# Reordering the products of a pair of k-blocks in a split-precision encoder block: high weight parts first, low parts last

## The chip, the cores and the metric

The kernel runs on one core of one Trainium2 chip. A core has a matrix engine (TensorE), a vector engine (VectorE), an activation engine (ScalarE), a general engine (GpSimd, POOL in the profile) and a queue that issues transfers (SyncE, SP). The metric is device time in microseconds (us) of one execution, lower is better. The median of three runs before the change is 2034.01 us (2033.57 to 2034.16).

## The reference, cut to what matters

One layer of an encoder: 256 tokens, width 4096, everything in float32. Five large weight matrices are streamed once.

```python
xn = rms_norm(h, norm_in_g[i])
proj = xn @ w_in[i]                          # 4096 x 14336
q, k, v, z_a, a_c, g_c, z_c = jnp.split(proj, ..., axis=-1)
y_a = chunked_attention(q, k, v, rel_table[i])
y_a = rms_norm(y_a, attn_out_g[i]) * jax.nn.silu(z_a)
y_c = conv_module(a_c, g_c, ..., w_pw[i], b_pw[i])   # 2048 x 2048 inside
y_c = rms_norm(y_c, conv_out_g[i]) * jax.nn.silu(z_c)
h = h + jnp.concatenate([y_a, y_c], axis=-1) @ w_out[i]        # 4096 x 4096
gate = jax.nn.sigmoid(rms_norm(h, ple_norm_g[i]) @ w_ple_gate[i] + b_ple_gate[i])
h = h + gate * (p[i] @ w_ple[i])
return rms_norm(h, final_g)
```

## The kernel before, in words

**Split products.** A float32 operand is held as the sum of a high part (a rounded format that TensorE multiplies in one pass) and a low part (what the rounding left). A product x @ w is then three matmuls: high x with high w, low x with high w, high x with low w, called kinds 0, 1 and 2 in the helper `add` (lines 378 to 389). The weight's high part is a cast by ScalarE (line 204), its low part a subtraction by VectorE that needs the high part (line 205); both are made in `parts_of`. There are three buffers each for high parts (`wh`) and low parts (`wl`), five for raw weights (`wt`), and two each for the parts of sums of blocks (`uh`, `ul`). A buffer comes free when its last reader is done. In a matmul the block of x (128 by 128) is the stationary operand, loaded by an instruction of its own (PEld in the profile), and 512 columns of w stream through it.

**Products.** `mixed_product` computes two column blocks of 512 for both halves of the tokens (256 tokens are two blocks of 128 rows), over all k-blocks in pairs. It holds four accumulators of 128 by 512, one bank each, with the names P2, P4, P3 and X; the pool `ps_acc` has four buffers, so the next product's four accumulators take the banks of this one. A *unit* of its list is one pair of k-blocks, done in one of two ways:
- a plain step: 8 block products, 24 matmuls, written by `add_plain` for one k-block and then the other; per block in the order of the column block j, the token half h, the kind;
- a seven-product step (marked `*` or `+` in the lists): a Strassen-like scheme with seven block products (P1, P5, P7, P2, P3, P6, P4), 21 matmuls, at the price of sums of weight blocks `ua` and `ub` on VectorE (lines 465 to 473; for `+` the first is formed by two transfers, one with accumulation, lines 418 and 419). P1, P5, P6 and P7 go to four helper banks of the pool `ps_tmp`.

The lists (`dense`, `early`, `first`, `late` and so on, lines 329 to 338) begin and end with plain steps. The first nine steps of the first product are written out in `first_pairs` by hand, with pinned order; the last product holds its last three pairs back and finishes them in pinned order (`add_left`).

**Reading out.** When a product ends, VectorE reads the four accumulators in the order of `QUARTERS` (P2, P4, P3, X) and combines each with sums from the helper banks: line 535 for scaled pairs, 1028 and 1030 for the pointwise product, 1054 for the gates, 1138 for the output projection, 1180 for the last gate. There are 25 such products on the four `ps_acc` banks: 9 scaled pairs (convolution inputs, queries and keys, values), 2 single value blocks by `product` (line 229), 2 pointwise, 4 gates, 4 of the output projection, 4 of the last gate; three of the last four are followed by `product` calls in `ps_tmp`.

**Order.** Except where `pin` keeps the program's order, a planner orders each engine's instructions when the program is built: it steps through a model of the engines, gives an engine the ready instruction that stands earliest in the program, and assigns a buffer when its tile is first written. So the program's order is a priority, and each engine's order is fixed before the run. On the chip each engine waits by semaphores for what its next instruction needs. Work that can be put off (convolution taps, normalisation) lies in a list `later`, of which `fill` issues a few after each step.

Of the kernel before, what the change touches and what calls it, by code (L numbers as in the profile page):

```python
# [25 lines left out]
def hybrid_block(  # L26
# [25 lines left out]
    NH = T // P  # L52
# [129 lines left out]
    def fill(n):  # L182
        for _ in range(min(n, len(later))):
            later.popleft()()
# [11 lines left out]
    def part_tiles():  # L196
        return [wpool.tile([P, KC, NB], F32R, tag=tag, name=tag, bufs=3) for tag in ("wh", "wl")]

    def parts_of(wt, kc, tiles=None):
        if tiles is None:  # L200
            tiles = part_tiles()
        wh, wl = tiles
        made = (
            nc.scalar.copy(wh[:, :kc, :], wt[:, :kc, :]),  # L204
            nc.vector.tensor_tensor(  # L205
                wl[:, :kc, :], wt[:, :kc, :], wh[:, :kc, :].bitcast(F32), ALU.subtract
            ),
        )
        recent[:] = made
        return (wh, wl), made  # L210
# [108 lines left out]
    def pair_parts(src):  # L319

        tiles = [upool.tile([P, 2, NB], F32R, tag=tag, name=tag) for tag in ("uh", "ul")]
        return parts_of(src, 2, tiles)[0]
# [17 lines left out]
    def mixed_product(  # L340
        w, col, lhs, comb, order, on_helpers, ahead=None, fills=(0,), on_begin=None, apart=NB,
# [36 lines left out]
        def add(name, x, w2, n, final, kinds=range(3), then=lambda ins: None):  # L378

            for kind in kinds:  # L380
                a, b = ((x[0], w2[0]), (x[1], w2[0]), (x[0], w2[1]))[kind]
                made.append(
                    nc.tensor.matmul(  # L383
                        banks[name], a, b, start=name not in begun,
                        stop=final and ends[name] == n and kind == 2 and not (left and name in "P2 P3 P4"),
                    )
                )
                begun.add(name)
                then(made[-1])

        def block(kb, h):
            t = lhs[kb // 4]
            return [t[:, kb % 4, q, h * P : (h + 1) * P] for q in range(2)]

        def add_plain(n, k, wh, wl, **kw):
            pair = order[n][0]
            for j in range(2):
                for h in range(NH):
                    name = (("P2", "P3"), ("P4", "X"))[h][j]
                    add(name, block(2 * pair + k, h), (wh[:, j], wl[:, j]), n, k == 1, **kw)  # L400

        sums = {}

        def sums_ahead(n):
# [22 lines left out]
        for n, (pair, seven) in enumerate(order):  # L427
# [4 lines left out]
            wts = []  # L432
            for k in range(2):
                wt = wpool.tile([P, 2, NB], F32, tag="w", name="wt")
# [10 lines left out]
                fill(fills[n % len(fills)])  # L445
                continue
            if not seven:
                for k in range(2):
                    add_plain(n, k, *parts_of(wts[k], 2)[0])
                fill(fills[n % len(fills)])  # L450
                continue
            begins = not helper
# [7 lines left out]
            w0h, w0l = parts_of(w0, 1)[0]  # L460
# [6 lines left out]
            with queued_behind(before if seven == "+" else ()):  # L467
                uah, ual = pair_parts(ua)
            w1h, w1l = parts_of(w1, 2)[0]
# [7 lines left out]
            def s_of(i):  # L477
                t, at = comb[pair] if isinstance(comb, dict) else (comb[pair // 4], pair % 4)
                return [t[:, at + i // 2, q, (i % 2) * P : (i % 2 + 1) * P] for q in range(2)]

            k0, k1 = 2 * pair, 2 * pair + 1
            add("P1", block(k0, 0), (w0h[:, 0], w0l[:, 0]), n, True)
            add("P5", s_of(1), (uah[:, 0], ual[:, 0]), n, True)
            add("P7", s_of(0), (uah[:, 1], ual[:, 1]), n, True)
            add("P2", block(k1, 0), (w1h[:, 0], w1l[:, 0]), n, True)
            add("P3", s_of(3), (w1h[:, 1], w1l[:, 1]), n, True)
            add("P6", s_of(2), (ubh[:, 0], ubl[:, 0]), n, True)
            add("P4", block(k1, 1), (ubh[:, 1], ubl[:, 1]), n, True)
            if begins and on_begin:
# [31 lines left out]
    def scaled_pair(w, col, apart, order, r, fills, home={}, **kw):  # L521

        t, z = [], []

        def on_helpers(helper):
            for dst, src in zip((t, z), sum_tiles(**home)):
                dst.extend(src)
            nc.scalar.activation(z[0][0], helper["P1"], AF.Identity, scale=r[:, :1])
            helper_sums(helper, z)
            for h, j in QUARTERS[1:]:  # L530
                nc.scalar.activation(z[h][j], z[h][j], AF.Identity, scale=r[:, h : h + 1])

        c = mixed_product(w, col, xT, xS, order, on_helpers, fills=fills, apart=apart, **kw)
        for h, j in QUARTERS:
            stt(
                z[h][j], c[h][j], r[:, h : h + 1], z[h][j],
                ALU.mult, ALU.subtract if j else ALU.add,
            )
        return t
# [682 lines left out]
    for j in range(2):  # L1222
        wt = wpool.tile([P, 2, NB], F32, tag="w", name="wt")
# [115 lines left out]
```

## Time and profile before

| what | value |
|---|---|
| median of three runs | 2034.01 us |
| profiled execution, its own time | 2032.83 us |
| its span, first to last instruction | 2031.1 us |
| mean granted TensorE clock | 0.998 |
| instructions | 26144 |
| TensorE matmuls, weight loads | 9094, 9094 |
| from HBM | 430.77 MB, 214 GB/s over the span |

In the profile PE is TensorE's matmuls, PEld its weight loads, DVE VectorE, ACT ScalarE, POOL GpSimd; L383 is line 383 of the kernel. Windows and starts are in us from the span's start. A group's row gives count, busy us, mean ns of one, then the engine's idle time just before and who ended it. A matmul's drawn length covers its way through the array, and the next one starts before it ends: the distance between starts is the rate.

### The profile page before, as it was taken

The numbers are of one execution on the slowest core, as the hardware profiler recorded it, in microseconds if no ns is written. First come the engines' busy times: TensorE is split into PE (matmuls) and PEld (weight loads), VectorE is DVE, ScalarE is ACT, GpSimd is POOL, SyncE is SP. The second block draws the span as 40 slices with busy tenths as digits, with TensorE's granted clock in tenths as the row PEclk, the third lists the DMA queues.
The fourth block names the chain that finished last, engine by engine and source line by source line (L and its number), as shares of the span: only waits on it lengthen the run. The fifth ranks groups of instructions, "written<-read, shape, count | busy, mean of one in ns | idle before, by whom it ended". The sixth has DMA issues, their size and how long they took to land.

```text
span 2031.1 us, 26144 instructions
## 1 busy us (share of the span) xinstructions
PE 2015.5 (99%) x9094; PEld 1658.7 (82%) x9094; DVE 1871.1 (92%) x2658; ACT 1203.3 (59%) x1568; POOL 46.0 (2%) x50
## 2 busy tenths in 40 slices
PE   9999999999999999999999999999999999999997
PEld 7888888888888888888888888888888888888876
DVE  7999999679999986868899999999999999999998
ACT  7655555655655445676556566675665666665555
POOL 0000000000000000000000000000000000000000
PEclk9999999999999999999999999999999999999999
DMA  8787878688678867556666666676666656666765
GB/s 294 223 237 233 257 214 251 191 245 239 188 217 250 254 187 207 171 185 205 194 214 198 202 205 214 217 229 209 206 213 201 208 187 207 204 220 205 234 208 179
DMA packets 171167, 436.69 MB, mean 215 GB/s; under 512 B 13966, under 2 KB 17182, under 8 KB 171034
## 3 DMA queue, kind: packets, MB, share of 16 engines
q1 hardware_dynamic: 161952, 417.93, 64.0%
q0 software_dynamic: 8432, 16.25, 4.9%
q8 instruction: 71, 1.16, 0.2%
q10 hardware_dynamic: 650, 0.84, 0.1%
q14 instruction: 62, 0.51, 0.1%
HBM read 430.77 MB, written 4.19 MB: 214 GB/s over the span
## 4 chain that ended last, share of the span: by engine, by line
PE 92%; DVE 5%; issue 2%; ACT 1%; DMA 1%; POOLq 0%; POOL 0%; ACTq 0%; DVEq 0%
PE acc L383 67%; PE acc_P L383 16%; PE acc L229 5%; DVE wl L205 2%; PE tmp_ps L170 1%; DVE cv L721 1%; DMA wt<-in_w_out_dram 0%; PE tmp_ps L890 0%; DVE ul L205 0%; PE tmp_ps L874 0%; PE tmp_ps L908 0%; PE tmp_ps L913 0%; ACT wh L204 0%; PE acc L371 0%; DVE cv L799 0%
## 5 line engine op out<-in xcount | busy, mean ns | idle before, releaser
L383 PE MATMUL acc<-wh,big_t 128*128 128x512 f32 x3992 | 1234.7, 391 | 0.7 <-DVE y_c L1030 0.3
L204 ACT CAST wh<-wt 128x1024 fp32r<-128x1024 f32 (+1 forms) x737 | 713.4, 978 | 550.5 <-PE acc L383 365.0
L205 DVE TENSOR_TENSOR wl<-wt,wh 128x1024 fp32r<-128x1024 f32 (+1 forms) x737 | 821.8, 1127 | 82.0 <-ACT wh L204 78.6
L383 PEld LDWEIGHTS acc<-wh,big_t 128*128 128x128 f32 x3992 | 746.8, 188 | 155.1 <-issue 0.9
L383 PE MATMUL acc<-wl,big_t 128*128 128x512 f32 x1996 | 770.7, 391 | 0.6 <-DVE wl L205 0.5
L383 PEld LDWEIGHTS acc<-wl,big_t 128*128 128x128 f32 x1996 | 374.3, 188 | 79.5 <-DVE wl L205 2.3
L204 ACT CAST uh<-ua 128x1024 fp32r<-128x1024 f32 x160 | 168.3, 1052 | 80.9 <-DVE ua L466 46.1
L721 DVE SCALAR_TENSOR_TENSOR cv<-uT,dw,cv 128x250 f32<-128x250 f32 (+19 forms) x480 | 202.3, 463 | 1.1
L205 DVE TENSOR_TENSOR ul<-ua,uh 128x1024 fp32r<-128x1024 f32 x160 | 194.9, 1218 | 8.4 <-ACT uh L204 8.0
L383 PE MATMUL acc_P<-uh,big_t 128*128 128x512 f32 x516 | 157.9, 391 | 0.0
L204 ACT CAST uh<-ub 128x1024 fp32r<-128x1024 f32 x92 | 96.8, 1053 | 95.8 <-DVE ub L473 86.5
L205 DVE TENSOR_TENSOR ul<-ub,uh 128x1024 fp32r<-128x1024 f32 x92 | 112.2, 1220 | 6.1 <-ACT uh L204 5.2
L383 PEld LDWEIGHTS acc_P<-uh,big_t 128*128 128x128 f32 x516 | 95.8, 188 | 22.3 <-ACT uh L204 3.1
L383 PE MATMUL acc_P<-ul,big_t 128*128 128x512 f32 x258 | 98.8, 391 | 0.1
L229 PE MATMUL acc<-wh,big_t 128*128 128x512 f32 x304 | 93.9, 390 | 0.0
L465 DVE TENSOR_TENSOR ua<-wt 128x512 f32<-128x512 f32 x95 | 65.1, 685 | 18.3 <-DMA wt<-in_w_in_dram 12.4
L383 PE MATMUL acc<-uh,big_t 128*128 128x512 f32 x252 | 78.1, 390 | 0.0
L383 PE MATMUL acc_P<-wh,big_t 128*128 128x512 f32 x252 | 77.8, 389 | 0.0
L229 PEld LDWEIGHTS acc<-wh,big_t 128*128 128x128 f32 x304 | 56.9, 188 | 11.9 <-issue 0.2
L383 PE MATMUL acc_P<-uh,comb_t 128*128 128x512 f32 x216 | 66.4, 390 | 0.1
L466 DVE TENSOR_TENSOR ua<-wt 128x512 f32<-128x512 f32 x95 | 64.9, 683 | 1.1 <-DMA wt<-in_w_in_dram 1.1
L473 DVE TENSOR_TENSOR ub<-ub,wt 128x512 f32<-128x512 f32 x92 | 63.0, 685 | 0.8
(250 smaller groups left out, 1589.3 us busy)
## 6 DMA issues: line engine op xcount, KB each, us to landing
wt<-in_w_in_dram SPq DMA_DIRECT2D x416, 512.0 KB, 4.5
wt<-in_w_out_dram SPq DMA_DIRECT2D x128, 512.0 KB, 4.3
wt<-in_w_ple_gate_dram SPq DMA_DIRECT2D x128, 512.0 KB, 4.2
wt<-in_w_pw_dram SPq DMA_DIRECT2D x32, 512.0 KB, 4.7
ua<-in_w_in_dram SPq DMA_DIRECT2D x31, 512.0 KB, 4.2
ua<-in_w_in_dram POOLq DMA_DIRECT2D x31, 512.0 KB, 8.3
wt<-in_w_in_dram SPq DMA_DIRECT2D x31, 256.0 KB, 2.7
hc<-in_x_dram SPq DMA_DIRECT2D x8, 512.0 KB, 4.8
```

What stands on the lines that cost most here:

```text
L170: nc.tensor.transpose(pt[:, i * T + h * P : i * T + (h + 1) * P], src[:, h, b] if len(src.shape) == 4 else src[:, h, b * P : (b + 1) * P], ...
L204: nc.scalar.copy(wh[:, :kc, :], wt[:, :kc, :]),
L205: nc.vector.tensor_tensor(wl[:, :kc, :], wt[:, :kc, :], wh[:, :kc, :].bitcast(F32), ALU.subtract),
L229: nc.tensor.matmul(acc, a, b[:, k, :], start=kb == 0 and kind == 0, stop=kb == kblocks - 1 and kind == 2,)
L383: nc.tensor.matmul(banks[name], a, b, start=name not in begun, stop=final and ends[name] == n and kind == 2 and not (left and name in "P2 ...
L465: plus(ua[:, 0], w0[:, 0], w0[:, 1])
L466: plus(ua[:, 1], w0[:, 1], w1[:, 1])
L473: plus(ub[:, 1], ub[:, 0], w1[:, 0])
L721: nc.vector.scalar_tensor_tensor(cv[:, i, PAD - k :], uT[:, i, : T + k - PAD], dw[:, b, k : k + 1], cv[:, i, PAD - k :], ALU.mult, ALU.add,)
```

## The change

The products of a pair of k-blocks are put in another order. In plain steps a new function `add_pair` takes the place of two calls of `add_plain`: first all 16 matmuls that read high parts of both blocks, then the 8 that read low parts; the loops run over block, token half, kind and column block, so that the two column blocks of one stationary operand follow each other. In seven-product steps the five products P1, P2, P3 (of raw blocks) and P5, P7 (of the first sum) are done with their high parts first (P1, P2, P3, then P5, P7) and then with their low parts in the same order; P6 and P4 follow as before. `add_plain` stays for the pinned first steps. The parts themselves, the buffers and the transfers are made by the same code in the same order.

```diff
+        def add_pair(n, parts):
+
+            pair = order[n][0]
+            for kinds in ((0, 1), (2,)):
+                for k, (wh, wl) in enumerate(parts):
+                    for h in range(NH):
+                        for kind in kinds:
+                            for j in range(2):
+                                name = (("P2", "P3"), ("P4", "X"))[h][j]
+                                add(name, block(2 * pair + k, h), (wh[:, j], wl[:, j]), n, k == 1, (kind,))
...
             if not seven:
-                for k in range(2):
-                    add_plain(n, k, *parts_of(wts[k], 2)[0])
+                add_pair(n, [parts_of(wt, 2)[0] for wt in wts])
                 fill(fills[n % len(fills)])
                 continue
...
-            add("P1", block(k0, 0), (w0h[:, 0], w0l[:, 0]), n, True)
-            add("P5", s_of(1), (uah[:, 0], ual[:, 0]), n, True)
-            add("P7", s_of(0), (uah[:, 1], ual[:, 1]), n, True)
-            add("P2", block(k1, 0), (w1h[:, 0], w1l[:, 0]), n, True)
-            add("P3", s_of(3), (w1h[:, 1], w1l[:, 1]), n, True)
+            raw = (
+                ("P1", block(k0, 0), (w0h[:, 0], w0l[:, 0])),
+                ("P2", block(k1, 0), (w1h[:, 0], w1l[:, 0])),
+                ("P3", s_of(3), (w1h[:, 1], w1l[:, 1])),
+            )
+            two = (
+                ("P5", s_of(1), (uah[:, 0], ual[:, 0])),
+                ("P7", s_of(0), (uah[:, 1], ual[:, 1])),
+            )
+            for group, kinds in ((raw, (0, 1)), (two, (0, 1)), (raw, (2,)), (two, (2,))):
+                for product_of in group:
+                    add(*product_of, n, True, kinds)
             add("P6", s_of(2), (ubh[:, 0], ubl[:, 0]), n, True)
             add("P4", block(k1, 1), (ubh[:, 1], ubl[:, 1]), n, True)
```

## The prediction

> **What bounds the kernel now.** I read the page's busy times first, then the chain, then the engines by stretch, to see whether TensorE is short of work anywhere. The next two fences are lines of the page (busy time and share; the chain by engine; the costliest group: count, busy us, mean ns, idle before it) and the busy times by stretch.
>
> ```profile
> PE 2015.5 (99%) x9094; PEld 1658.7 (82%) x9094; DVE 1871.1 (92%) x2658; ACT 1203.3 (59%) x1568; POOL 46.0 (2%) x50
> PE 92%; DVE 5%; issue 2%; ACT 1%; DMA 1%; POOLq 0%; POOL 0%; ACTq 0%; DVEq 0%
> L383 PE MATMUL acc<-wh,big_t 128*128 128x512 f32 x3992 | 1234.7, 391 | 0.7 <-DVE y_c L1030 0.3
> ```
>
> ```profile
> 0.00:50.00 50.00, 48.70 (x234) 38.57 (x235) 36.40 (x61) 36.45 (x70) 0.88 (x8) 1.00 0.86 294
> 50.00:1980.00 1930.00, 1928.49 (x8681) 1588.90 (x8680) 1793.47 (x2537) 1140.44 (x1460) 43.29 (x40) 1.00 0.69 214
> 1980.00:2031.00 51.00, 38.32 (x183) 31.27 (x181) 41.28 (x61) 26.37 (x39) 1.86 (x2) 0.92 0.52 179
> 1200.00:1300.00 100.00, 100.00 (x443) 82.71 (x442) 95.19 (x114) 58.96 (x65) 0.00 (x0) 1.00 0.63 205
> ```
>
> TensorE carries 92% of the chain. Of its 15.6 us of idle time, 14.0 lie in the first 50 us and the last 51 us, which the change does not reach; 1.5 are left between. The granted clock there is 1.00. A busy TensorE can still hide delay, though, because a matmul is drawn 391 ns long while the next starts sooner. So I looked at one place where it did wait (matmuls, VectorE, weight loads; start, length, and in brackets the idle time with who ended it):
>
> ```profile
> 838.51 1.98 PE L383 MATMUL acc<-wh,big_t 128*128 128x512 f32 x8
> 841.01 1.20 PE L383 MATMUL acc<-wl,big_t 128*128 128x512 f32 x4 [0.53 <-DVE wl L205]
> 839.75 2.35 DVE L205 TENSOR_TENSOR wl<-wt,wh 128x1024 fp32r<-128x1024 f32 x2
> 841.01 0.77 PEld L383 LDWEIGHTS acc<-wl,big_t 128*128 128x128 f32 x4 [0.95 <-DVE wl L205]
> ```
>
> Eight starts in 1.98 - 0.39 us make a pitch of 0.227 us for seven steps. The ninth matmul was due at 838.51 + 8 x 0.227 = 840.33 and started at 841.01: 0.68 us lost. The next three take 0.81 us instead of 0.68: a restart costs 0.13 more. Also, eight products with high parts stand in a row here, against the program's order (two high, one low): the planner already pulls high products forward where it sees a low part late. The change writes by hand what the planner does in need.
>
> **The change part by part.** No instruction is added or removed: 9094 matmuls, 9094 loads, the same casts and subtractions, the same DMAs on SP's and POOL's queues in the same program order. What moves is when parts are needed and when buffers and banks come free. I count in matmuls of 0.227 us; the lists of units give 214 plain steps of 24 matmuls that pass through the new function, and 126 seven-product steps of 21.
>
> (a) *Low parts are needed later* (plain step: the 17th and 21st matmul in place of the 3rd and 15th; seven-product step: w0's 11th in place of 3rd, ua's 14th in place of 6th, high ua 7th in place of 4th). This can give back what is now lost to late parts. Those waits, of the matmuls and then of the weight loads (total us, times, longest):
>
> ```profile
> PE acc L383 <- DVE wl L205: 0.5, 1, 0.5
> PE acc L383 <- DVE y_c L1030: 0.3, 1, 0.3
> PE acc L383 <- DVE z L1054: 0.2, 1, 0.2
> PE acc_P L383 <- DVE ul L205: 0.2, 1, 0.2
> PEld acc_P L383 <- ACT uh L204: 3.9, 14, 0.5
> PEld acc_P L383 <- DVE ul L205: 2.8, 9, 0.6
> PEld acc L383 <- DVE wl L205: 2.3, 5, 0.9
> ```
>
> The true loss lies between the matmuls' idle time (wl 0.5 + ul 0.2 = 0.7) and the loads' (3.9 + 2.8 + 2.3 = 9.0), since the wait at 841 cost 0.68 + 0.13 beside 0.53 of the one and 0.95 of the other. P6 and P4, whose place does not move, keep their part of it. I take a gain of 4; the ends are 0.7 and 9.
>
> (b) *High parts are needed earlier.* The worst is w1 of a seven-product step, from the 10th matmul to the 3rd, 7 x 0.227 = 1.6 us. A cast of it, the step's start and its first use now:
>
> ```profile
> 1203.23 1.04 ACT L204 CAST wh<-wt 128x1024 fp32r<-128x1024 f32 x1
> 1205.68 0.62 PE L383 MATMUL acc_P<-wh,big_t 128*128 128x512 f32 x2
> 1207.72 0.62 PE L383 MATMUL acc<-wh,big_t 128*128 128x512 f32 x2
> ACT wh L204 <- PE acc L383: 365.0, 276, 3.3
> ```
>
> The cast ends at 1204.27 and the new order wants it at 1205.68 + 0.45 = 1206.13: 1.9 us in hand. The last row says that ScalarE stands waiting for a high buffer 276 times; those buffers now come free 4 matmuls (first block) and 8 matmuls (second) sooner. Cost 0; if that lead were gone, at most 1.6 us in each of 126 steps.
>
> (c) *Low buffers are held longer:* in a plain step the first block's until the 20th matmul in place of the 12th, 1.8 us. There are three, so the subtraction that takes this buffer serves the block three further on, and from release to need 15 matmuls are left at the tightest place (w1 of the seven-product step that follows), 3.4 us for 1.22 us of VectorE. I take 0; the other end is a rival. The raw tile is released by that subtraction, and SP's loads stand behind it:
>
> ```profile
> SPq L438 <- DVE wl L205: 1047.9, 497, 9.8
> DVE ua L465 <- DMA wt<-in_w_in_dram: 12.4, 11, 2.4
> ```
>
> VectorE waits for arriving weights in 11 places only, 12.4 us that TensorE did not feel; I take 0 here too, to 2 us.
>
> (d) *The hand-over between products.* This is where I expect the cost. A product fills four banks, and all four are needed by the next product's first step. Before, the last plain step ended its banks at matmuls 15, 18, 21, 24 and the next began with them at 1, 4, 7, 10: nine matmuls between last and first use of each. Now they end at 21, 22, 23, 24 and are wanted at 1, 2, 5, 6: three for the first two. Three hand-overs as they are (TensorE's last matmul of the first bank, where shown, and its next start; VectorE's reads, four in a row):
>
> ```profile
> 96.54 0.39 PE L383 MATMUL acc<-wl,big_t 128*128 128x512 f32 x1
> 98.81 0.61 PE L383 MATMUL acc<-wh,big_t 128*128 128x512 f32 x2
> 97.05 2.78 DVE L535 SCALAR_TENSOR_TENSOR z<-acc,r_x,z 128x512 f32<-128x512 f32 x4 [1.35 <-PE acc L383]
> 182.29 0.39 PE L383 MATMUL acc<-wl,big_t 128*128 128x512 f32 x1
> 184.56 0.62 PE L383 MATMUL acc<-wh,big_t 128*128 128x512 f32 x2
> 182.87 2.72 DVE L535 SCALAR_TENSOR_TENSOR z<-acc,r_x,z 128x512 f32<-128x512 f32 x4
> 1154.56 0.70 PE L383 MATMUL acc<-wh,big_t 128*128 128x512 f32 x2
> 1152.59 1.22 DVE L205 TENSOR_TENSOR ul<-ua,uh 128x1024 fp32r<-128x1024 f32 x1
> 1153.73 2.48 DVE L1054 TENSOR_TENSOR z<-acc,z 128x512 f32<-128x512 f32 x4
> L1054 DVE TENSOR_TENSOR z<-acc,z x16: 677/680/684, 1072.0 to 1323.1; 128x512 f32<-128x512 f32 x16
> L535 DVE SCALAR_TENSOR_TENSOR z<-acc,r_x,z x36: 729/744/753, 97.0 to 852.7; 128x512 f32<-128x512 f32 x36
> ```
>
> At 97 VectorE was idle, so its read starts as early as it can: 97.05 - 96.54 = 0.51 us after the start of the matmul that it waits for. One read takes 0.744 us, the four follow 0.68 us apart. At 1154 VectorE came late: its first read (0.680 by the row of L1054) ended at 1154.41, and TensorE went on at 1154.56, 0.15 later. Call the next product's start T. The first bank's last product now starts at T - 4 x 0.227 = T - 0.91, the read at T - 0.40, ends at T + 0.34, and TensorE goes on at T + 0.49. In strict order the second bank, read 0.68 later, adds 0.68 - 0.23 = 0.45; if the planner puts more products of the first bank ahead, nothing. Restart 0.13. So 0.6 to 1.1 us with VectorE free, and up to 1.2 more if it is inside a subtraction, as at 1152.59. I take 0.8, in the lower part, because the planner was seen to reorder.
>
> There are 19 such hand-overs (25 products, less the two single ones, the three followed by products in other banks, and the last). In 12 nothing else stands ready; in 7 (attention, transposes) I take 0.3. That makes 12 x 0.8 + 7 x 0.3 = 11.7, less 0.7 that hand-overs cost already (the matmul waits on y_c and z above, 0.5, and a restart each): 11.0. Bounds: 2 (planner fills nearly all) to 19 x 1.9 = 36.
>
> The last product ends in blocks that are held and written out by hand, and the first nine steps are pinned: 0 for both.
>
> **Sum.** 11.0 - 4 = +7.0 on the profiled execution's 2032.83 us (span 2031.1): 2039.8. The three runs' median, 2034.01, is 1.2 above it: 2041.0.
>
> **A rule weighed: one load for two products.** In the new plain step two matmuls in a row use the same stationary block. The nearest rows of two matmuls with the same block are the warm-up's, and matmuls of half width give the fixed part of a pitch:
>
> ```profile
> L125 PEld LDWEIGHTS <-idle x10: 102/151/151, 1.2 to 5.4; 128*128 128x128 bf16 x10
> L125 PE MATMUL tmp_ps<-idle x10: 380/634/634, 1.2 to 5.6; 128*128 128x512 bf16 x10
> 2015.10 1.24 PE L371 MATMUL part<-big_t 128*128 128x256 f32 x9
> ```
>
> Ten matmuls with one block made ten loads: nothing is merged, and a load lies beside the matmul before it. Were it merged, the most to win is the fixed part: (1.24 - 0.28) / 8 = 0.120 us at 256 columns, so 2 x 0.120 - 0.227 = 0.013 us in 214 x 12 = 2568 matmuls, 33 us. The Trainium skill, "TensorE: Matmul & The Clock Gate", Part 2, step 1, says that decoupling the load lets you "load once and matmul repeatedly"; by that rule, with the same page's 2.5 ns floor, the estimate would be some 28 us less than before. The ten loads for ten matmuls speak against it here.
>
> **The rivals.**
> - *The hand-over is covered, no change.* The planner gives TensorE the first bank's four high products, or P1 and P5 of the next seven-product step, while VectorE reads. For it: the eight high products at 838. Against it: helper products follow only in lists that have a seven-product step second, not in the early ones, and nothing can start before T + 0.49. Cost (d) is then about 4, equal to gain (a): 2034.
> - *Late parts were the dearer thing, faster.* (a) gives its whole 9 and (d) costs 3: 2034.0 - 6 = 2028. It decides when (d) stays under 0.2 us a hand-over. Against it: TensorE's own idle time on parts is 0.7.
> - *One load for two products, faster:* 2034 - 33 = 2001.
> - *VectorE blocked by low buffers, much slower.* The plan has a subtraction at the head of VectorE's queue waiting for a buffer until the 20th matmul, and everything behind it waits too. Between 1200 and 1300 VectorE has 4.8 us free and some 10 plain steps; if half of the 1.8 us reaches it in each, 9 - 4.8 = 4.2 us are lost per 100 us, over the dense 900 us 38: 2072. It decides from a quarter on. Against it: the 3.4 us window of (c), and that every other low part has a later deadline.
>
> **How the numbers follow.** Hand-over as reckoned 0.60; covered 0.26; late parts 0.07; one load 0.02; low buffers 0.05. Likeliest: 2041.0, its own range 2036 to 2052. Eight in ten need the no-change case too: 2031 to 2053. A difference of 0.2%, 4.1 us, is about what a measurement can tell from none: faster 0.09, same 0.26, slower 0.65.
>
> **What the profile after would show.** If I am right: VectorE's reads of acc (L535, L1028 to L1054 and so on shifted) preceded by idle time that TensorE ends, in more than the two places of before; TensorE or its loads waiting for z, hc and y_c several us in sum; waits on wl and ul nearly gone; the count of loads 9094. Wrong if the waits on z, hc and y_c stay under 2 us in sum, if loads get fewer, or if VectorE waits for TensorE ahead of wl in hundreds of places.

## The result and the profile after

The changed kernel takes 2061.95 us (median of 4 runs, 2059.96 to 2063.99) where the kernel before, on the same chip, takes 2034.09 (4 runs, 2033.57 to 2034.28): the ratio is 1.0138, with a 95% interval of 1.0123 to 1.0154. It is 27.9 us slower. The prediction was 2041.0 with a range of 2031 to 2053: the sign was right, and the time lies 9 us above the range.

The profiled execution took 2062.42 us, its span is 2060.6, and the mean granted clock is 0.998 as before. The first fence holds lines of the page after the change (busy times, the chain by engine, TensorE's two costliest groups with count, busy us, mean ns, idle before them), the second its busy times by stretch (start to last, matmuls, weight loads, VectorE, ScalarE, GpSimd, then clock and DMA share).

```profile
PE 2021.8 (98%) x9094; PEld 1657.1 (80%) x9094; DVE 1871.8 (91%) x2658; ACT 1199.0 (58%) x1568; POOL 57.8 (3%) x50
PE 84%; DVE 10%; issue 3%; DMA 2%; ACT 1%; DVEq 0%; POOLq 0%; POOL 0%; ACTq 0%; SPq 0%
L383 PE MATMUL acc<-wh,big_t 128*128 128x512 f32 x3992 | 994.6, 392 | 11.0 <-DVE z L552 5.9
L383 PE MATMUL acc<-wl,big_t 128*128 128x512 f32 x1996 | 526.8, 391 | 7.2 <-DVE wl L205 7.2
```

```profile
0.00:50.00 50.00, 48.81 (x234) 38.47 (x235) 36.20 (x61) 36.16 (x70) 0.88 (x8) 1.00 0.87 293
50.00:2010.00 1960.00, 1935.08 (x8680) 1587.07 (x8679) 1794.02 (x2538) 1136.47 (x1460) 55.02 (x40) 1.00 0.67 211
2010.00:2061.00 51.00, 37.87 (x183) 31.59 (x181) 41.59 (x61) 26.32 (x40) 1.87 (x2) 0.90 0.52 180
```

The work is the same: 9094 matmuls, 9094 loads, 2658 instructions of VectorE. The two ends of the span are unchanged. In the middle TensorE's idle time went from 1.5 us to 1960 - 1935.08 = 24.9, and VectorE's part of the chain from 5% to 10%. Who ended that idle time is in the waits (engine and tile that waited, whom for: total us, times, longest):

```profile
PE acc L383 <- DVE wl L205: 7.2, 6, 1.6
PE acc L383 <- DVE z L552: 5.9, 5, 1.7
PE tmp_ps L891 <- DVE z L552: 4.0, 3, 1.5
PE acc L383 <- DVE z L1071: 2.0, 2, 1.1
PE acc L383 <- ACT wh L204: 1.9, 3, 1.0
PE acc L383 <- DVE y_c L1045: 0.9, 1, 0.9
DVE wl L205 <- PE acc L383: 19.2, 17, 3.1
DVE ua L475 <- DMA wt<-in_w_out_dram: 17.0, 9, 4.1
DVE ua L475 <- DMA wt<-in_w_in_dram: 12.5, 9, 2.6
```

Two families show. TensorE waits for the reads of finished accumulators (z, y_c: 5.9 + 4.0 + 2.0 + 0.9 = 12.8 us in these rows), and it waits for low parts of weights (wl: 7.2, where it was 0.5). Behind both, VectorE itself has new waits: 17 times a subtraction stands at the head of its queue until TensorE frees a buffer, a row that the profile before did not have with `acc`; and its waits for weights of the output projection went to 17.0 us, the longest 4.1, from this row of before:

```profile
DVE ua L465 <- DMA wt<-in_w_out_dram: 4.4, 8, 1.7
```

Idle time leaves out restarts and whatever the drawn length of a matmul covers, so I also counted from starts: for each matmul after the first 8 us, the distance to the start before it less the pitch of that width (0.227 us at 512 columns, 0.120 at 256, 0.109 or 0.110 for narrower ones), where that is over 0.03 us, put down to what ended the wait. The sums, in us, from the trace of the profiled execution:

| lost by TensorE at starts | before | after |
|---|---|---|
| low parts (wl, ul) | 1.8 | 8.8 |
| reads of accumulators (z, y_c, hc) | 1.2 | 16.1 |
| high parts (wh, uh) | 0.5 | 4.4 |
| transfer of `pin` | 0 | 1.3 |
| other waits | 1.8 | 2.7 |
| no wait shown (restarts, pitch) | 15.9 | 17.8 |
| total | 21.3 | 51.0 |
| span less total | 2009.8 | 2009.6 |

The last row closes the account: without what TensorE loses at starts the two spans agree within 0.2 us. (The executions differ by 2062.42 - 2032.83 = 29.6, the medians by 27.9.) So the whole difference lies in when TensorE may start.

**One hand-over, read closely.** The timeline around the first hand-over, start, length, engine, and in brackets the idle time before with who ended it:

```profile
97.02 1.98 PE L383 MATMUL acc<-wl,big_t 128*128 128x512 f32 x8
100.21 3.87 PE L383 MATMUL acc<-wh,big_t 128*128 128x512 f32 x16 [1.22 <-DVE z L552]
98.18 1.23 DVE L205 TENSOR_TENSOR wl<-wt,wh 128x1024 fp32r<-128x1024 f32 x1 [3.08 <-PE acc L383]
99.32 2.72 DVE L552 SCALAR_TENSOR_TENSOR z<-acc,r_x,z 128x512 f32<-128x512 f32 x4
```

The next product was due at 97.02 + 8 x 0.227 = 98.83 and started at 100.21: 1.38 us lost. The first bank gets its last product at 97.02 + 4 x 0.227 = 97.93, so its read could have begun 0.51 later, at 98.44, as the prediction found. But one matmul earlier, with the 20th of the step at 97.70, the low buffer of the first block came free, and the subtraction that waited for it, planned ahead of the read, began at 98.18 and held VectorE for 1.23 us. The read began at 99.32 and ended 0.744 later at 100.06; TensorE went on 0.15 after that. Without the subtraction it would have been 98.44 + 0.744 + 0.15 = 99.33, 0.50 lost. Of the nine hand-overs of scaled pairs eight have such a subtraction right ahead of the first read; by the starts, seven of these lost 1.38 to 1.84 us and the eighth, where matmuls of the attention came in between (at 362), 0.83. The ninth, without it, lost 0.57.

**One late low part, read closely.** A seven-product step of the output projection:

```profile
1482.97 0.39 PE L383 MATMUL acc_P<-wl,big_t 128*128 128x512 f32 x1
1484.99 0.74 PE L383 MATMUL acc<-wl,big_t 128*128 128x512 f32 x2 [1.62 <-DVE wl L205]
1481.37 0.69 DVE L475 TENSOR_TENSOR ua<-wt 128x512 f32<-128x512 f32 x1 [4.06 <-DMA wt<-in_w_out_dram]
1481.98 1.22 DVE L205 TENSOR_TENSOR ul<-ub,uh 128x1024 fp32r<-128x1024 f32 x1
1483.71 2.35 DVE L205 TENSOR_TENSOR wl<-wt,wh 128x1024 fp32r<-128x1024 f32 x2
```

TensorE has the low part of the first raw block (the `acc_P` line) and stands before that of the second. The subtraction that makes it starts at 1483.71, behind ul (1481.98), behind the first sum `ua` of a later step (1481.37), which stood 4.06 us at the head of VectorE's queue until its raw weights arrived. The high part that this subtraction needs was already in use by TensorE at 1481.16. The low part is late because VectorE takes its queue in order and something that nobody needed yet stood in front. Six such places between 612 and 1652 us, each behind a first sum that waited for its weights, make 8.2 of the 8.8.

### The profile page after: what moved, and what is told of

Same layout as the page of the kernel before. It is cut to its first block, busy times and chain, and to the rows that moved or that the text cites. A ratio compares the mean times of both kernels' runs of the same rounds, so it can differ in the third digit from the quotient of the medians.

```text
span 2060.6 us, 26152 instructions
## 1 busy us (share of the span) xinstructions
PE 2021.8 (98%) x9094; PEld 1657.1 (80%) x9094; DVE 1871.8 (91%) x2658; ACT 1199.0 (58%) x1568; POOL 57.8 (3%) x50
## 4 chain that ended last, share of the span: by engine, by line
PE 84%; DVE 10%; issue 3%; DMA 2%; ACT 1%; DVEq 0%; POOLq 0%; POOL 0%; ACTq 0%; SPq 0%
PE acc L383 62%; PE acc_P L383 14%; PE acc L229 5%; DVE wl L205 4%; DVE ul L205 1%; DMA wt<-in_w_ple_gate_dram 1%; PE tmp_ps L170 1%; DVE hc L184 1%; DMA wt<-in_w_out_dram 1%; DVE ua L476 0%; DVE cv L738 0%; DVE ub L483 0%; DVE ua L475 0%; PE tmp_ps L891 0%; DVE ub L482 0%
## 5 line engine op out<-in xcount | busy, mean ns | idle before, releaser
L383 PE MATMUL acc<-wh,big_t 128*128 128x512 f32 x3992 | 994.6, 392 | 11.0 <-DVE z L552 5.9
L205 DVE TENSOR_TENSOR wl<-wt,wh 128x1024 fp32r<-128x1024 f32 (+1 forms) x737 | 812.4, 1129 | 94.9 <-ACT wh L204 51.6
L383 PE MATMUL acc<-wl,big_t 128*128 128x512 f32 x1996 | 526.8, 391 | 7.2 <-DVE wl L205 7.2
L738 DVE SCALAR_TENSOR_TENSOR cv<-uT,dw,cv 128x250 f32<-128x250 f32 (+24 forms) x480 | 202.2, 466 | 1.0
L383 PE MATMUL acc_P<-uh,big_t 128*128 128x512 f32 x516 | 146.8, 391 | 0.6 <-ACT uh L204 0.6
L229 PE MATMUL acc<-wh,big_t 128*128 128x512 f32 x304 | 94.1, 390 | 0.4 <-DVE z L552 0.4
L383 PE MATMUL acc_P<-ul,big_t 128*128 128x512 f32 x258 | 87.1, 392 | 0.2
L482 DVE TENSOR_TENSOR ub<-ua,wt 128x512 f32<-128x512 f32 x92 | 63.0, 685 | 0.2
```

The costliest lines, as they stand in the source:

```text
L205: nc.vector.tensor_tensor(wl[:, :kc, :], wt[:, :kc, :], wh[:, :kc, :].bitcast(F32), ALU.subtract),
L229: nc.tensor.matmul(acc, a, b[:, k, :], start=kb == 0 and kind == 0, stop=kb == kblocks - 1 and kind == 2,)
L383: nc.tensor.matmul(banks[name], a, b, start=name not in begun, stop=final and ends[name] == n and kind == 2 and not (left and name in "P2 ...
L482: plus(ub[:, 0], ua[:, 0], w1[:, 1])
L738: nc.vector.scalar_tensor_tensor(cv[:, i, PAD - k :], uT[:, i, : T + k - PAD], dw[:, b, k : k + 1], cv[:, i, PAD - k :], ALU.mult, ALU.add,)
```

## The experiments

Twelve kernels. Each ratio, and each difference with a plus sign, is against the kernel before run on the same chip; its median there was 2033.2 to 2034.2.

**The hand-over alone.** The kernel before, with only the last plain step of each product in the new order.

```diff
-                for k in range(2):
-                    add_plain(n, k, *parts_of(wts[k], 2)[0])
+                if n + 1 == len(order):
+                    add_pair(n, [parts_of(wt, 2)[0] for wt in wts])
+                else:
+                    for k in range(2):
+                        add_plain(n, k, *parts_of(wts[k], 2)[0])
```

> The kernel before with one edit: only the last plain step of each product goes through the new function; the other plain steps and all seven-product steps keep the old order. Hand-over theory: the four banks end together, so the time goes up by what TensorE waits at the ends of products in the changed kernel, about 15 to 16 us (z, y_c and hc in its waits), to 2050. Rival, low buffers (the loss lies in low parts held over many steps in a row): at most 3 us, 2037.

Measured 2049.92 us (2047.77 to 2050.55), ratio 1.0078 [1.0063, 1.0093]: +15.7 us, as expected. More than half of the 27.9 comes from the one step in which the order decides when banks come free. Its waits and its first hand-over:

```profile
PE acc L383 <- DVE z L549: 5.6, 5, 1.3
PE acc L383 <- DVE z L1068: 1.4, 2, 0.7
```

```profile
98.55 1.98 PE L383 MATMUL acc<-wl,big_t 128*128 128x512 f32 x8
99.71 1.23 DVE L205 TENSOR_TENSOR wl<-wt,wh 128x1024 fp32r<-128x1024 f32 x1 [2.46 <-PE acc L383]
100.85 0.74 DVE L549 SCALAR_TENSOR_TENSOR z<-acc,r_x,z 128x512 f32<-128x512 f32 x1
```

The same picture as in the full change: the 20th matmul starts at 98.55 + 3 x 0.227 = 99.23, the subtraction begins 0.48 later, and the read comes behind it. The subtraction stands right ahead of the read at five of the nine scaled pairs; at three others convolution taps stand there, which hold the read back at 275 (0.88 lost) and hardly at 541 and 721 (0.52 each). So the time came out as expected, but not all of it where expected: by starts the reads cost about 11.5 us, some 10 more than before, and the profiled span is 17.7 longer. The rest lies in other places, such as high parts of sums (0.94 at 1802 and again at 1980) and low parts (3.1 in all).

**The other half: the change with the last plain step in the old order.**

```diff
-                add_pair(n, [parts_of(wt, 2)[0] for wt in wts])
+                if n + 1 == len(order):
+                    for k in range(2):
+                        add_plain(n, k, *parts_of(wts[k], 2)[0])
+                else:
+                    add_pair(n, [parts_of(wt, 2)[0] for wt in wts])
```

> The changed kernel with the last plain step of each product in the old order again. Hand-over theory: 15 to 16 us come back, 2046. Low buffers: about nothing comes back, 2058 to 2062. If the hand-over were all of the loss: 2034.

Measured 2052.27 (2049.96 to 2055.19), ratio 1.0096 [1.0079, 1.0113]. Only 9.7 us came back, so the expectation missed: the new order costs some 18 us even where every product ends as before. Its rows:

```profile
PE acc L383 <- DVE wl L205: 6.9, 8, 1.9
PE acc L383 <- DVE z L1075: 2.0, 3, 0.8
```

The late low parts are all still there (8.2 us by starts), and reads in the gates are late although their banks end in the old order (3.8 by starts), because VectorE comes late to them.

**Seven-product steps alone, and plain steps alone.** In the first, the changed kernel has `add_pair` taken out again:

```diff
-                add_pair(n, [parts_of(wt, 2)[0] for wt in wts])
+                for k in range(2):
+                    add_plain(n, k, *parts_of(wts[k], 2)[0])
```

> The order of the seven-product steps alone; plain steps as before. If the late low part of w1 (8 us in the changed kernel) comes from the plain steps' longer hold on low buffers: within 3 us of before, 2031 to 2037. If it comes from the order inside the seven-product step: 8 to 12 us more, 2042 to 2046.

Measured 2041.73 (2039.84 to 2045.54), ratio 1.0042 [1.0027, 1.0057]: +7.5, just below the second range that I gave. The seven-product order makes late low parts by itself, and late reads too: by starts the profiled execution (2045.54, the slowest of the four) loses 5.5 us on low parts and 5.7 on reads of accumulators, mostly in the gates. Waits, then one of the places (SPq is SP's own queue, four transfers issued):

```profile
DVE ua L476 <- DMA wt<-in_w_in_dram: 25.4, 11, 4.2
DVE ua L476 <- DMA wt<-in_w_out_dram: 12.1, 7, 3.3
PE acc L383 <- DVE z L1072: 3.8, 5, 0.9
PE acc L383 <- DVE wl L205: 3.1, 4, 1.2
```

```profile
1204.68 11.57 SPq L449 DMA_DIRECT2D wt<-in_w_in_dram  x4
1212.94 0.69 DVE L476 TENSOR_TENSOR ua<-wt 128x512 f32<-128x512 f32 x1 [4.21 <-DMA wt<-in_w_in_dram]
1214.68 1.22 DVE L205 TENSOR_TENSOR wl<-wt,wh 128x1024 fp32r<-128x1024 f32 x1
1215.96 0.73 PE L383 MATMUL acc<-wl,big_t 128*128 128x512 f32 x2 [1.05 <-DVE wl L205]
```

It is the chain of 1482 again, here with its origin: SP, whose loads wait for the subtraction that frees a raw tile, issued loads at 1202.34, 1204.68, 1206.42 and 1207.02, the last two 0.6 us apart. The one of 1206.42 landed at 1212.85, 6.4 us later, and the one of 1207.02 took 7.1, where the median for these loads is 4.6; VectorE's `ua` had waited 4.21 us for the first of the two.

In the second, the changed kernel has the five products of a seven-product step written as before:

```diff
-            for group, kinds in ((raw, (0, 1)), (two, (0, 1)), (raw, (2,)), (two, (2,))):
-                for product_of in group:
-                    add(*product_of, n, True, kinds)
+            add("P1", block(k0, 0), (w0h[:, 0], w0l[:, 0]), n, True)
+            add("P5", s_of(1), (uah[:, 0], ual[:, 0]), n, True)
...
```

> The order of the plain steps alone; seven-product steps as before. Hand-over and low buffers both lie in plain steps, so by that theory nearly all of the loss: 2055 to 2062. If the seven-product order makes the late low parts: 2050.

Measured 2055.94 (2053.28 to 2057.0), ratio 1.0107 [1.0092, 1.0122]: +21.8, at the lower edge of the first range. The two halves add up to 7.5 + 21.8 = 29.3, near the whole. Its rows:

```profile
PE acc L383 <- DVE z L545: 5.9, 5, 1.7
PE acc L383 <- DVE wl L205: 2.6, 4, 1.4
DVE wl L205 <- PE acc L383: 40.5, 23, 3.8
```

Of the 21.8 the last step alone makes 15.7; the other 6 are the inner plain steps. By starts they are spread over reads, low parts, high parts, the transfer of `pin` and restarts, none by more than some 2 us. No run cuts them further; that they hang on the low buffers held longer is made likely by the block-by-block runs below, which do not hold them longer.

**Do the low buffers carry it? Six shared buffers.** The change, with high and low parts drawn from one set of six in place of three and three. The memory is the same; what is gone is the fixed number of low ones.

```diff
-        return [wpool.tile([P, KC, NB], F32R, tag=tag, name=tag, bufs=3) for tag in ("wh", "wl")]
+        return [wpool.tile([P, KC, NB], F32R, tag="part", name=tag, bufs=6) for tag in ("wh", "wl")]
```

> The changed kernel with one edit: high and low parts share six buffers in place of three and three, so a low part that is held long no longer stops the next one. If the late low parts come from the three low buffers: VectorE's waits for TensorE ahead of wl (19 us) and TensorE's waits on wl (8 us) go, the hand-over's 16 us stay, 2048 to 2052. If they come from the order that the planner chose (first sums of a later step placed ahead, waiting for their transfer): 2058 to 2062.

Measured 2046.45 (2043.98 to 2047.2), ratio 1.0061 [1.0046, 1.0076]: +13.0, so some 15 us of the 27.9 are gone, more than expected. Rows:

```profile
PE acc_P L383 <- ACT wh L204: 4.0, 7, 1.3
PE acc L383 <- ACT wh L204: 3.4, 5, 2.1
PE acc L383 <- DVE z L552: 1.2, 2, 0.9
DVE wl L205 <- PE acc L383: 44.8, 29, 3.6
```

Waits of matmuls on wl are gone, and reads of the scaled pairs cost 3.8 in place of 11.9 us by starts. In their place TensorE waits for high parts (9.5 us by starts): low parts now sit in buffers that high parts want. Two of the three signs that I had named did not come: the hand-over's 16 us did not stay, and VectorE's waits for TensorE ahead of wl did not go, they went from 19.2 to 44.8 us. A subtraction still waits for a buffer, but at the first hand-over for one that comes free with the 16th matmul of the last step, the last that reads a high part, and not with the 20th. It begins at 97.15 and is done when the first bank is, and 0.50 us are lost where it was 1.38, as reckoned above for a hand-over without the subtraction. The loads come apart too: 6 loads of weights were issued within 0.8 us of the one before, where the changed kernel has 40, and VectorE's waits for weights fell from 36.8 to 22.5 us.

**And on the kernel before?** The same line is changed there, and nothing else:

```diff
-        return [... tag=tag, name=tag, bufs=3) for tag in ("wh", "wl")]
+        return [... tag="part", name=tag, bufs=6) for tag in ("wh", "wl")]
```

> The kernel before with six shared buffers for high and low parts: what the edit of the shared run does without the change. 2030 to 2036 if the three and three never bound it; above 2040 if sharing lets high parts crowd out low ones.

Measured 2035.62 (2034.53 to 2037.18, 10 runs), ratio 1.0011 [1.0002, 1.002]. Sharing is no gain of its own; it costs about 2 us (0.4 to 4 by the interval). What it does for the changed kernel is to undo part of the change's harm.

**Seven-product order with six shared buffers.** The seven-product order alone, with the shared set:

```diff
-                add_pair(n, [parts_of(wt, 2)[0] for wt in wts])
+                for k in range(2):
+                    add_plain(n, k, *parts_of(wts[k], 2)[0])
...
-        return [... tag=tag, name=tag, bufs=3) for tag in ("wh", "wl")]
+        return [... tag="part", name=tag, bufs=6) for tag in ("wh", "wl")]
```

> The order of the seven-product steps alone, with six shared buffers for high and low parts. If its 7.5 us come from w0's and the sum's low parts standing in their buffers longer (later subtractions, raw blocks freed late and in bunches, loads late): back to 2033 to 2038. If the order itself costs (high parts of w1 wanted sooner, banks in turn): 2040 to 2044.

Measured 2038.43 (2037.12 to 2040.31, 8 runs), ratio 1.0026 [1.0016, 1.0037], just past the upper edge of what I expected. Against the kernel before on that chip (2033.2) it is +5.2 where it was +7.5; less the 2 that sharing costs by itself, about 3 of the 7.5 remain. It supports the buffers as the larger part and does not prove them the whole.

**Seven-product order with the first block's low part kept early.** A finer cut: P1, the only product that uses the parts of the first raw block, does its three matmuls at the start, so that block's low buffer is free after the 3rd matmul and not the 11th. The other high products come one matmul later by it; all else is as in the seven-product order alone.

```diff
-            for group, kinds in ((raw, (0, 1)), (two, (0, 1)), (raw, (2,)), (two, (2,))):
+            for group, kinds in ((raw[:1], (0, 1, 2)), (raw[1:], (0, 1)), (two, (0, 1)), (raw[1:], (2,)), (two, (2,))):
```

> The order of the seven-product steps alone, but P1 keeps its three matmuls together at the start, so that w0's low buffer is free after the 3rd matmul as before, in place of the 11th. If w0's low buffer is what the loss hangs on: 2033 to 2038. If it is the other low parts or the order: 2040 to 2044.

Measured 2035.7 (2033.9 to 2037.35, 10 runs), ratio 1.0011 [1.0001, 1.0021]: +2.5, as expected. Five of the 7.5 us hang on this edit, which lets one buffer go eight matmuls (1.8 us) sooner. The waits of VectorE for arriving weights fell with it:

```profile
DVE ua L476 <- DMA wt<-in_w_in_dram: 6.7, 6, 2.1
DVE ua L476 <- DMA wt<-in_w_out_dram: 3.9, 4, 1.9
PE acc L383 <- DVE wl L205: 1.2, 2, 0.7
```

25.4 + 12.1 us of waiting for weights became 6.7 + 3.9, and the matmuls' wait for wl 3.1 became 1.2. By starts the reads of accumulators cost 1.8 us where it was 5.7. The loads are issued as close together as before: 20 within 0.8 us of the one before, landing after 5.9 us at the median, against 22 and 6.0. So loads close together do not make the loss by themselves. Whether the low buffer itself or the raw tile behind it is the tighter link was not tried alone.

**Plain steps block by block.** The order within a plain step with the loops over block and kind of `add_pair` exchanged (the cut is against the change): each block's high products, then its low ones. The first block's low buffer comes free at the 12th matmul again; the banks still end at 21 to 24. Seven-product steps as before.

```diff
-            for kinds in ((0, 1), (2,)):
-                for k, (wh, wl) in enumerate(parts):
+            for k, (wh, wl) in enumerate(parts):
+                for kinds in ((0, 1), (2,)):
```

> Plain steps with the loops over block and kind exchanged: 8 products with high parts and 4 with low parts of the first block, then of the second. Seven-product steps as before. A low buffer is held no longer than before, the banks of the last step still end together (21st to 24th), the pairs with one stationary operand are kept. Hand-over theory: the same as the last step alone, 2050. If the order inside the other plain steps (pairs, banks in turn) costs by itself: 2055 or more.

Measured 2045.2 (2044.13 to 2046.13), ratio 1.0057 [1.0042, 1.0072]: +11.7, some 5 less than the 2050 expected. This is the hand-over without a subtraction that waits until the 20th matmul. Its first one:

```profile
99.03 1.07 PE L383 MATMUL acc<-wl,big_t 128*128 128x512 f32 x4
99.54 2.07 DVE L545 SCALAR_TENSOR_TENSOR z<-acc,r_x,z 128x512 f32<-128x512 f32 x3 [0.68 <-PE acc L383]
100.44 0.70 PE L383 MATMUL acc<-wh,big_t 128*128 128x512 f32 x2 [0.34 <-ACT wh L204]
```

The first of the four low products is the first bank's last one: read 0.51 later, next product at 100.44 where 99.03 + 4 x 0.227 = 99.94 was due. That is 0.50 lost, what the prediction's formula gives (the profile puts the wait down to a cast that ended at about the same time as the read). Where VectorE is free the loss is 0.42 to 0.50. At four scaled pairs a convolution tap stands ahead of the read, and 0.79 to 1.25 are lost; at the first product of the pointwise stage, at 955, two instructions on `y_c` stand there and 2.31 are lost. So with three matmuls between last and first use it is not the subtraction alone that costs: whatever stands ahead of the read in VectorE's queue does.

**The same, with the last plain step in the old order.** The cut is against the run before.

```diff
-                add_pair(n, [parts_of(wt, 2)[0] for wt in wts])
+                if n + 1 == len(order):
+                    for k in range(2):
+                        add_plain(n, k, *parts_of(wts[k], 2)[0])
+                else:
+                    add_pair(n, [parts_of(wt, 2)[0] for wt in wts])
```

> As the run before, with the last plain step of each product in the old order. Neither long hold nor common end of the banks is left: 2031 to 2037, no change. If pairs or alternating banks cost by themselves: 2040 or more.

Measured 2033.85 (2033.19 to 2035.45, 10 runs), ratio 1.0003 [0.9994, 1.0013]: no change. This kernel does the two column blocks of one stationary operand one after the other in nearly all plain steps, and moves high products ahead of low ones within each block. Neither is worth anything that can be measured, and neither costs anything, once the low buffer and the banks come free as before.

**High parts first, but the banks ended one after the other.** The kernel before, with another last plain step, put in as in the first experiment: all 16 high products first, as in the change, then the low ones bank by bank, so that the banks end at matmuls 18, 20, 22 and 24 and not at 21 to 24.

```diff
...
+            for j in range(2):
+                for h in range(NH):
+                    for k, (wh, wl) in enumerate(parts):
+                        name = (("P2", "P3"), ("P4", "X"))[h][j]
+                        add(name, block(2 * pair + k, h), (wh[:, j], wl[:, j]), n, k == 1, (2,))
...
```

> Only the last plain step of each product differs from the kernel before: its 16 products with high parts, then the 8 with low parts bank by bank in the order in which VectorE reads (ends at the 18th, 20th, 22nd, 24th). High parts first and low parts last are kept, only the banks end in turn again. Hand-over theory: the first bank has 6 matmuls in place of 3 until the next product, VectorE's read fits, 2033 to 2038. If low parts last cost there whatever the banks do: 2045 to 2050.

Measured 2036.53 (2035.72 to 2038.19, 10 runs), ratio 1.0016 [1.0007, 1.0026]: +3.3, as expected. Its first hand-over:

```profile
96.65 1.98 PE L383 MATMUL acc<-wl,big_t 128*128 128x512 f32 x8
97.38 2.73 DVE L553 SCALAR_TENSOR_TENSOR z<-acc,r_x,z 128x512 f32<-128x512 f32 x4 [2.03 <-PE acc L383]
98.47 0.63 PE L383 MATMUL acc<-wh,big_t 128*128 128x512 f32 x2
```

The first bank's last product is the second low one, which starts at 96.88; the read begins 0.50 later and ends at 98.12, and the next product starts at 98.47 = 96.65 + 8 x 0.227, on time. The first experiment (+15.7) differs from this one only in the order of its eight low products, and some 12 us turn on it. Two things moved at once: the first bank ends earlier, and the first block's low buffer comes free later, with the 23rd matmul, so that its subtraction now stands behind the first read. The block-by-block order, in which no such subtraction stood ahead, shows that the distance costs by itself: three matmuls between a bank's last product and its next first use are too few even for a free VectorE, and six are enough for it. Where VectorE is not free, six are not enough either: in the pointwise stage and the gates of this kernel, between 947 and 1160, four reads still come 0.6 to 0.9 us late, behind work for sums of blocks or on `y_c`.

**Both remedies on the changed kernel:** six shared buffers and the last plain step in the old order.

```diff
-        return [... tag=tag, name=tag, bufs=3) for tag in ("wh", "wl")]
+        return [... tag="part", name=tag, bufs=6) for tag in ("wh", "wl")]
...
+                if n + 1 == len(order):
+                    for k in range(2):
+                        add_plain(n, k, *parts_of(wts[k], 2)[0])
+                else:
+                    add_pair(n, [parts_of(wt, 2)[0] for wt in wts])
```

> The changed kernel with both cures: last plain step of each product in the old order, six shared buffers. If hand-over and low buffers are all of the loss: 2033 to 2038. If something else is left: 2040 or more.

Measured 2038.21 (2037.1 to 2040.03, 9 runs), ratio 1.0026 [1.0016, 1.0036]: +5.0, between the two ranges. About 23 of the 28 us are gone; of what is left, the row below and the 2 us that sharing costs by itself are the larger part.

```profile
PE acc L383 <- ACT wh L204: 2.8, 3, 2.1
```

No order that was tried beats the kernel before; the block-by-block one with the old last step equals it.

## Why the prediction was right and where it was wrong

**Sign and site: right.** The prediction put the cost at the hand-over between products, and the first experiment, which changes that place alone, costs +15.7. That the work itself costs the same (9094 matmuls and loads, span less lost time the same within 0.2 us) was right too.

**Step (d), the hand-over: right mechanism, mis-sized.** Predicted +11.0, measured by starts 16.1 - 1.2 = +14.9. The formula for a free VectorE, T + 0.49, held (0.50 in the block-by-block order), and the pieces 0.51, 0.744 and 0.15 held to the hundredth. What failed is the choice of 0.8 "in the lower part, because the planner was seen to reorder". The prediction had written down the other end, "up to 1.2 more if it is inside a subtraction", but did not carry over to the hand-over what it writes under *VectorE blocked by low buffers*: that a subtraction stands at the head of VectorE's queue until the 20th matmul. The first bank is done with the 21st, so such a subtraction goes ahead of the read. Those two numbers side by side would have given 1.4 and not 0.8 for such a hand-over. In the changed kernel eight of the nine scaled pairs have it so, and in all the nine cost 11.9 us. The planner did not fill the gap: seven of them lost 1.38 to 1.84. Nor did the 0.3 hold for hand-overs with other work at hand: at 274, 541 and 724 the transposes that would have filled the gap need the same read (the row of L891) and 1.38 to 1.62 were lost.

Two things came out better than the working. The 0.45 for the second bank was not paid: TensorE did 16 products in a row once the first bank was read (100.21). It was also reckoned for the wrong bank, since P3, wanted with the 2nd matmul, is the third that VectorE reads, which in strict order would add 2 x 0.68 - 0.23 = 1.13. And the hand-overs of the output projection lost only 0.1 to 0.2 each. That the hand-over alone cost +10 by starts in the first experiment, near the predicted 11.0, is in part luck: fewer hand-overs had the subtraction, and those that had it cost more than 0.8.

**Step (a), "low parts are needed later", a gain of 4: failed.** Loss on low parts went from 1.8 to 8.8 us, +7 in place of -4. That is 11 of the 22.8 us by which the sum of 7.0 fell short of the 29.8 by which the loss at starts grew, the largest single error. A later deadline helps only if the part is made at the same time as before; at the six places read above it was made later.

**Step (c), "low buffers are held longer", reckoned at 0: failed, and with it (a).** The prediction counted from the release of a buffer to the next need of it, found 3.4 us for a subtraction of 1.22, and stopped. It saw the row of VectorE's waits for weights (12.4 us "that TensorE did not feel") and took "0 here too, to 2 us". What the runs show in its place is a longer chain: low buffer freed later, subtraction later, raw tile freed later, load later and close behind another, transfer landing later, VectorE standing at a first sum for up to 4 us, and the next low part queued behind that. Undoing the first link, the first raw block's low buffer in seven-product steps, returned 5 of 7.5 us; giving the parts a common set of buffers returned some 15 of 27.9, part of it at the hand-over. That the chain runs through all of these links is read from the traces; the links were not each cut alone, and one of them is in doubt: with the first link undone the loads came as close together as before, and two thirds of the loss were gone all the same.

**Step (b), "high parts are needed earlier", cost 0: mis-sized.** It cost 4.4 - 0.5 = 3.9 us, most of it at one place in each of three products of the last gate (1.19 us at 1812, 0.6 at 1901 and at 1990, and 0.39 each at the sums' high parts right behind), in the middle of the product and not at a hand-over. The casts that end these waits had themselves waited for their weights (0.71 us at 1811.02, 0.21 at 1899.96, 0.22 at 1988.98), so the transfers were late there. The 1.9 us in hand was measured at 1204, in a stage where it holds; the last gate was not looked at, and no run was made for it. The late transfer of `pin` (1.3 us) and more restarts (1.9) are what remains, follow-on costs that the prediction had no term for.

**The rivals.** *Covered* fell by the first experiment, *late parts were the dearer thing* by the rows on wl. *One load for two products* fell three times: the loads are 9094 as before; the warm-up's ten matmuls with one block still make ten loads;

```profile
L125 PEld LDWEIGHTS <-idle x10: 103/151/152, 1.2 to 5.4; 128*128 128x128 bf16 x10
```

and the block-by-block order with the old last step, which has these pairs nearly everywhere, measures 1.0003. The rule from the Trainium skill, "TensorE: Matmul & The Clock Gate", Part 2, step 1 (load once, matmul repeatedly) does not come about here from order alone: no run shows a saved load. *VectorE blocked by low buffers*, given 0.05, was nearest in time (2072 against 2061.95) and in cause: VectorE's queue does stand behind a subtraction that waits for a buffer. But it stands there 17 times, not in every step, and the harm is done by what is queued behind it.

**What the profile was to show.** Of the signs named, several us of waits on z, hc and y_c came, and the loads stayed at 9094. "Waits on wl and ul nearly gone" did not come. Idle time of VectorE ahead of its reads of acc did not come either: it is there, but ahead of the subtraction that stands before the read.

## What to carry to other kernels

When an order moves the last use of a buffer, follow what waits for that buffer to its end: the instruction that takes it, what that instruction frees, the transfer behind that, and all that stands in the same in-order queue; a window that is long enough for one link says nothing of the chain. Compare at the seam between two products which release comes first: a 1.23 us instruction that became ready one matmul ahead of an urgent read made 1.38 us of loss out of 0.50. Count the matmuls between a bank's last product and its next first use, and look at what stands ahead of the read; here three cost 0.4 to 0.5 us with a free engine and up to 1.8 at the scaled pairs behind something else, and six cost nothing at the hand-over shown, where the engine was free.

## What the hardware showed that was not expected

- Loads issued close together landed late in these traces: in the seven-product order alone the 22 loads of weights that SP issued within 0.8 us of the one before landed after 6.0 us at the median, all loads of weights after 4.4; in the changed kernel it was 5.1 (40 of them) against 4.4. It shows as a wait of VectorE or ScalarE before it is one of TensorE.
- Starts of TensorE at which the records show no wait still lost 15.9 us before and 17.8 after. Restarts are a part of that (0.13 at the one in the prediction); what the rest is was not settled.
- TensorE's busy share moved from 99% to 98% while 29.8 us more were lost at starts. Its idle time shows 23 of these (15.6 to 38.8); the other 6 count as busy (2015.5 to 2021.8), since a matmul is drawn 0.39 us long and its successor is due after 0.227.
